# Attention scores of a two-layer decoder in 64-row products: heads by turns, three passes, and two bias transfers

## The chip, the cores and the metric

The kernel runs on one core of a Trainium2 chip. The metric is the device time of one execution in microseconds (us). Five engines work side by side, each through its own instructions in order: TensorE (PE; its weight loads are shown apart, as PEld), VectorE (DVE), ScalarE (ACT), GpSimd (POOL) and SyncE (SP), which here only issues transfers.

## What is computed

Two decoder layers over 256 positions of width 1024. Layer 0 mixes positions with a gated MLP, layer 1 with causal attention of 12 heads of 64. In both, 4 more heads of 64 attend to 256 memory tokens. Each layer ends in a SwiGLU block. Cut to what matters here:

```python
def memory_cross_attention(q_mem, mem, w_kv):            # 4 heads of 64, in both layers
    k, v = jnp.split(mem @ w_kv, 2, axis=-1)
    s = jnp.einsum('bshd,bmhd->bhsm', q, k) * HEAD_DIM ** -0.5
    return jnp.einsum('bhsm,bmhd->bshd', jax.nn.softmax(s, axis=-1), v)

# layer 0: u * (W_s v + b) by groups; layer 1: causal attention, 12 heads of 64
sub = jnp.concatenate([mix, mem_out], axis=-1) @ w_mix_out[i]
x = layer_norm(ALPHA * x + sub, ...)
x = layer_norm(ALPHA * x + swiglu(x, w_ffn_in[i], w_ffn_out[i]), ...)
```

## The kernel before, in words

Every large product is made of three passes. An operand is split into a rounded part hi and a rest lo, and hi·hi + lo·hi + hi·lo is added up in one PSUM tile. The helper `split` does that: ScalarE copies hi (L376), VectorE subtracts to get lo (L377). Weights are streamed from memory by SP in blocks of 128 x 2048, in an order written out by hand, split half by half (`spl_...` tiles), and used by PE (`mm`, L401). PE's order is that of the code. The orders of VectorE, ScalarE and SP are three long tables of numbers, `VECTOR_ORDER`, `SCALAR_ORDER` and `SYNC_ORDER`, which `keep_order` turns into dependencies.

The stages by time in the profile: the v projection of layer 0 (`va`, from 5.5 us), memory queries `hqm`, the u projections `pu`, memory keys `hkm`, the gating products `sv`, the memory scores `sm` (near 58 us), output projection `opa` (from 64 us), the feed-forward block (104 to 272 us, tiles Xf, Zf, fof and others), then layer 1: values `bv`, queries `hqm`, memory scores `sm` (near 303 us), six rounds of `qk` projection, scores `s`, transposes `pt` and `pv` (300 to 363 us), output projection `opc`, and the second feed-forward block (to 545 us).

The scores are the place of the change. Heads come in pairs, since two heads of 64 fill 128 rows. The scores do not use three passes over 64 rows. `stack_q` (L628, L629) writes, for each head of a pair, a tile whose one half of the rows holds hi and whose other half holds lo of the head's queries, times 0.125. `stack_k` (L636, L637, L638) writes the keys' hi into both halves of one tile and their lo into one half of another, `klm`, whose other half POOL has set to zero once at the start (L426). Two products over 128 rows then give all three terms: stacked queries by doubled hi keys, and stacked queries by `klm`. Every step of the stacking works on 64 rows: for a pair, two ScalarE and two VectorE steps for the queries, four ScalarE and two VectorE steps for the keys. In layer 1 this is done for six pairs (`qks`, by `qk_half`; `scores` issues 8 products a pair), in both layers for two pairs of memory heads (`qqm`, `kkm`; `mem_scores` issues 16 products a layer). The softmax then runs on VectorE and ScalarE, `pt` or `ptm` turns the result, and `pv` or `pvm` multiplies it with the values, two heads to a tile, in products 64 columns wide.

The gating of layer 0 adds a bias, `bs`. It is loaded by four transfers that spread one row over 64 partitions each, beside one transfer for the gating weights `wsT`. The tile `mix` holds the mixer's results, split, for the output projection.

Of the kernel before, what the change touches and what calls it, by code (L numbers as in the profile page):

```python
# [21 lines left out]
P = 128  # L22
D = 1024
T = 256
# [15 lines left out]
NEG = -1e30  # L40
BIG = 3e38
# [151 lines left out]
class Stream:  # L193
# [27 lines left out]
    def load_ahead(self):  # L221

        while self.loaded < len(self.units):
            name, n = self.units[self.loaded]
            tag = self.tag(name)
            if tag:
                if tag in self.held:
                    return
                self.held.add(tag)
                raw = self.actp.tile([P, 2, D], F32, tag=tag, name=f"raw_{name}").rearrange("p a c -> p (a c)")  # L230
            else:
                if sum(self.left[r] > 0 for r in self.ring) >= RAW_BUFS:
                    return
                self.ring.append(name)
                raw = self.rawp.tile([P, 2048], F32, tag="raw", name=f"raw_{name}")
            self.raw[name] = raw
            self.nc.sync.dma_start(raw[:, :n], self.unit_ap(block(name)))
            self.loaded += 1
# [80 lines left out]
)  # L319
SCALAR_ORDER = (  # L320
# [882 lines left out]
```

## Time and profile before

| | |
|---|---|
| time, median of 3 runs | 562.05 us (561.79 to 562.11) |
| the profiled execution | 561.61 us, span from first to last instruction 559.9 us |
| PE busy | 549.4 us, 98%, 3035 products |
| DVE busy | 504.6 us, 90%, 697 instructions |
| ACT busy | 388.1 us, 69%, 605 instructions |
| POOL busy | 48.4 us, 9% |
| transfers | 121.01 MB, mean 216 GB/s |

In the profile a name such as `s<-qks` is the tile written and the tiles read. `128*64` behind a product is the part of the array, rows by columns, that holds its weights. Products overlap, so the length of one is longer than the distance to the next. The chain is the work that ended last, followed back from the end, each step to what released it.

### The profile page before, as it was taken

The numbers are of one execution on the slowest core, as the hardware profiler recorded it, in microseconds if no ns is written. First come the engines' busy times: TensorE is split into PE (matmuls) and PEld (weight loads), VectorE is DVE, ScalarE is ACT, GpSimd is POOL, SyncE is SP. The second block draws the span as 40 slices with busy tenths as digits, with TensorE's granted clock in tenths as the row PEclk, the third lists the DMA queues.
The fourth block names the chain that finished last, engine by engine and source line by source line (L and its number), as shares of the span: only waits on it lengthen the run. The fifth ranks groups of instructions, "written<-read, shape, count | busy, mean of one in ns | idle before, by whom it ended". The sixth has DMA issues, their size and how long they took to land.

```text
span 559.9 us, 8132 instructions
## 1 busy us (share of the span) xinstructions
PE 549.4 (98%) x3035; PEld 475.6 (85%) x3035; DVE 504.6 (90%) x697; ACT 388.1 (69%) x605; POOL 48.4 (9%) x61
## 2 busy tenths in 40 slices
PE   9999999999999999999999999999999999999994
PEld 8999779988888888888899989787888888888884
DVE  5889957799998999999998878768999999999997
ACT  4767749975867769585466998768767687767720
POOL 1011002010202011100000000000202020201001
PEclk9999999999999999999999999999999999999998
DMA  8998665437969968778568243553379887988802
GB/s 304 384 382 289 245 266 123 178 63 174 292 173 331 250 247 202 267 222 323 165 244 357 77 151 121 145 122 142 66 222 274 294 214 244 271 238 249 253 6 77
DMA packets 23464, 121.01 MB, mean 216 GB/s; under 512 B 2688, under 2 KB 4736, under 8 KB 13312
## 3 DMA queue, kind: packets, MB, share of 16 engines
q1 hardware_dynamic: 17088, 99.16, 47.2%
q0 software_dynamic: 5760, 20.97, 21.0%
q8 instruction: 24, 0.39, 0.3%
q10 hardware_dynamic: 576, 0.34, 0.2%
q14 instruction: 16, 0.13, 0.1%
HBM read 119.42 MB, written 1.05 MB: 215 GB/s over the span
## 4 chain that ended last, share of the span: by engine, by line
PE 84%; DMA 6%; DVE 5%; issue 2%; ACT 2%; SPq 0%; POOLq 0%; POOL 0%; ACTq 0%; DVEq 0%
PE fof L401 11%; PE Xg L401 10%; PE Xf L401 10%; PE fog L401 9%; PE Zf L401 7%; PE Zg L401 7%; PE qk L401 6%; PE opc L401 4%; PE opa L401 3%; PE bv L401 3%; DMA raw_o<-in_w 2%; PE pg L401 2%; PE pf L401 2%; DMA raw_qm<-in_w 2%; PE pvm L401 2%
## 5 line engine op out<-in xcount | busy, mean ns | idle before, releaser
L376 ACT CAST spl_s_M<-raw_s_T 128x1024 fp32r<-128x1024 f32 x80 | 82.1, 1051 | 30.4 <-DVE raw_s_T L255 27.6
L377 DVE TENSOR_TENSOR spl_s_M<-raw_s_T,spl_s_M 128x1024 fp32r<-128x1024 f32 x80 | 95.9, 1219 | 2.1 <-ACT spl_s_M L376 2.1
L376 ACT CAST spl_s_M<-raw_s 128x1024 fp32r<-128x1024 f32 x60 | 61.5, 1051 | 19.0 <-DMA raw_s<-in_w 13.6
L377 DVE TENSOR_TENSOR spl_s_M<-raw_s,spl_s_M 128x1024 fp32r<-128x1024 f32 x60 | 71.3, 1220 | 3.3 <-ACT spl_s_M L376 3.3
L401 PE MATMUL fof<-spl_w,htf 128*128 128x512 f32 x264 | 63.0, 391 | 0.0
L401 PEld LDWEIGHTS fof<-spl_w,htf 128*128 128x128 f32 x264 | 49.4, 188 | 10.1
L377 DVE TENSOR_TENSOR spl_w<-raw_w,spl_w 128x1024 fp32r<-128x1024 f32 x44 | 53.5, 1220 | 0.9 <-ACT spl_w L376 0.9
L401 PE MATMUL fog<-spl_w,htg 128*128 128x512 f32 x228 | 54.2, 390 | 0.0
L401 PEld LDWEIGHTS fog<-spl_w,htg 128*128 128x128 f32 x228 | 42.8, 188 | 8.8
L255 DVE TENSOR_TENSOR raw_s_T<-raw_s_T,raw_s 128x1024 f32<-128x1024 f32 x40 | 48.3, 1220 | 0.2
L376 ACT CAST spl_w<-raw_w 128x1024 fp32r<-128x1024 f32 x44 | 45.7, 1053 | 0.1
L401 PE MATMUL qk<-x2T,spl_qk 128*128 128x256 f32 x288 | 36.6, 284 | 0.0
L219 POOL DMA_DIRECT2D raw_s<-in_w x20 | 17.1, 856 | 217.3 <-DVE spl_s_M L377 139.9
L401 PEld LDWEIGHTS qk<-x2T,spl_qk 128*128 128x128 f32 x288 | 35.2, 192 | 0.6 <-DVE klm L638 0.4
L401 PE MATMUL Xg<-spl_s_M,SgM 128*128 128x512 f32 x120 | 29.4, 394 | 0.0
L401 PE MATMUL Xf<-spl_s_M,SfM 128*128 128x512 f32 x120 | 29.3, 394 | 0.0
L401 PE MATMUL Xg<-spl_s_M,x3T 128*128 128x512 f32 x120 | 29.3, 392 | 0.0
L401 PE MATMUL Xf<-spl_s_M,x1T 128*128 128x512 f32 x120 | 28.9, 390 | 0.0
L401 PE MATMUL Zf<-spl_s_M,SfM 128*128 128x512 f32 x120 | 28.8, 390 | 0.0
L401 PE MATMUL Zg<-spl_s_M,SgM 128*128 128x512 f32 x120 | 28.8, 390 | 0.0
L401 PEld LDWEIGHTS Xg<-spl_s_M,x3T 128*128 128x128 f32 x120 | 22.4, 188 | 5.4 <-DVE x3T L377 0.4
L219 POOL DMA_DIRECT2D raw_s_T<-in_w x20 | 17.3, 865 | 108.9 <-DVE mb L551 74.7
(264 smaller groups left out, 1102.8 us busy)
## 6 DMA issues: line engine op xcount, KB each, us to landing
raw_w<-in_w SPq DMA_DIRECT2D x22, 1024.0 KB, 6.8
raw_s<-in_w SPq DMA_DIRECT2D x20, 1024.0 KB, 6.9
raw_s_T<-in_w SPq DMA_DIRECT2D x10, 1024.0 KB, 5.3
raw_s_T<-in_w POOLq DMA_DIRECT2D x20, 512.0 KB, 7.5
raw_s<-in_w POOLq DMA_DIRECT2D x20, 512.0 KB, 5.6
raw_o<-in_w SPq DMA_DIRECT2D x8, 1024.0 KB, 8.3
raw_qk<-in_w SPq DMA_DIRECT2D x6, 1024.0 KB, 4.8
raw_v<-in_w SPq DMA_DIRECT2D x7, 512.0 KB, 7.6
```

What stands on the lines that cost most here:

```text
L219: self.nc.gpsimd.dma_start(self.raw[name][:, sl], self.unit_ap(other)[:, sl], accum_op=ALU.add)
L255: self.nc.vector.tensor_add(raw, raw, self.raw[used[1]][:, sl])
L376: nc.scalar.copy(hi, src)
L377: nc.vector.tensor_sub(lo, src, hi.bitcast(F32))
L401: nc.tensor.matmul(o, lhsT, rhs, start=start, stop=stop, skip_group_check=on)
```

## The change

The stacking goes. `split_q` writes hi and lo of a pair's queries, both heads at once, in one ScalarE and one VectorE step over 128 rows, and `split` does the same for the keys. The scores are three passes (hi·hi, lo·hi, hi·lo) over 64 rows each: head 0 of the pair lies on rows 0 to 63, head 1 on rows 64 to 127, and the products of the two heads alternate, each into its own score tile. A pair in layer 1 takes 12 products where it took 8, the memory heads of a layer 24 where they took 16. `klm` and its two memsets on POOL go. VectorE has 20 instructions fewer, ScalarE 40 fewer. In `mem_scores` the softmax of a pair starts after the products of both heads.

The bias is spread over the partitions ahead of the launch: two thirds of it stand behind the gating weights and come in their transfer, the rest in one of its own, so five transfers become two. Three weight blocks, `qm0`, `u0` and `km0`, are loaded in two halves each, so SP's count stays the same. The three tables are new throughout; their numbers tell nothing by themselves.

```diff
+IN_HALVES = ("qm0", "u0", "km0")
...
-            self.nc.sync.dma_start(raw[:, :n], self.unit_ap(block(name)))
+            parts = 2 if name in IN_HALVES else 1
+            for x in range(parts):
+                sl = slice(x * n // parts, (x + 1) * n // parts)
+                self.nc.sync.dma_start(raw[:, sl], self.unit_ap(block(name))[:, sl])
...
 SYNC_ORDER = (
-    0, 1, 2, 3, 4, 5, 7, 6, 8, 9, 10, 11, 15, 16, 12, 17, 21, 13, 19, 18, 24, 23, 14, 22, 25, 26, 20, 27, 28, 29, 33,
+    1, 0, 2, 3, 4, 18, 5, 6, 7, 8, 9, 11, 10, 22, 12, 13, 14, 16, 15, 19, 17, 23, 20, 24, 25, 26, 21, 27, 28, 29, 32,
...
-        klm = const.tile([P, 2, 2, T], F32R, name="klm")
-        for par in range(2):
-            nc.gpsimd.memset(klm[HD - HD * par:2 * HD - HD * par, :, par, :].bitcast(F32), 0.0)
...
-        def mem_scores(qa, k, nm, psum_tile):
-            ka, kl = k
+        def mem_scores(qa, ka, nm, psum_tile):
             pr = []
-            for h in range(4):
-                c, par = h // 2, h % 2
-                s = psum_tile[h](f"s{nm}{h}")
-                for lo in range(2):
+            for c in range(2):
+                ss = [psum_tile[2 * c + par](f"s{nm}{2 * c + par}") for par in range(2)]
+                for n, (a, b) in enumerate(LO_LAST):
                     for q in range(2):
-                        mm(s[:, q * 256:(q + 1) * 256], qa[c][:, par, q * P:(q + 1) * P], (kl[:, c] if lo else ka[c])[:, par, :],
-                           not lo and not q, bool(lo and q))
-                pr.append(Softmax(s, [(0, 256), (256, 512)], f"{nm}{h}"))
+                        for par, s in enumerate(ss):
+                            mm(s[:, q * 256:(q + 1) * 256], qa[c][rows(par), a, q * P:(q + 1) * P], ka[c][rows(par), b, :],
+                               not n and not q, bool(n == 2 and q))
+                pr += [Softmax(s, [(0, 256), (256, 512)], f"{nm}{2 * c + par}") for par, s in enumerate(ss)]
...
-        def stack_q(qa, t):
-
-            for par in range(2):
-                own, other = rows(par)
-                nc.scalar.mul(qa(par)[own], t[own], 0.125)
-                nc.vector.scalar_tensor_tensor(qa(par)[other], t[own], 0.125, qa(par)[own].bitcast(F32),
-                                               ALU.mult, ALU.subtract)
-
-        def stack_k(ka, kl, t):
-
-            for par in range(2):
-                own, other = rows(par)
-                nc.scalar.copy(ka(par)[own], t[own])
-                nc.scalar.copy(ka(par)[other], t[own])
-                nc.vector.tensor_sub(kl[own, par], t[own], ka(par)[own].bitcast(F32))
+            return slice(HD * par, HD * par + HD)
+
+        def split_q(hi, lo, t):
+
+            nc.scalar.mul(hi, t, 0.125)
+            nc.vector.scalar_tensor_tensor(lo, t, 0.125, hi.bitcast(F32), ALU.mult, ALU.subtract)
...
-        nc.sync.dma_start(wsT, ins["wsT"])
+        nc.sync.dma_start(wbig, ins["wsT"])
...
-        for t, c, g0, g1 in ((wbig, 12 * P, 0, 4), (vbig, 12 * P, 4, 6)):
-            for j in range(2):
-                nc.sync.dma_start(t[j * HD:(j + 1) * HD, c:c + (g1 - g0) * P].rearrange("p (g t) -> p g t", t=P),
-                                  ins["bs"][j:j + 1, g0:g1, :].to_broadcast([HD, g1 - g0, P]))
+        nc.sync.dma_start(vbig[:, 12 * P:14 * P], ins["bs"])
...
-                stack_q(lambda par: st[:, 0, par, :], t)
+                split_q(qks[hp][:, 0, 0, :], qks[hp][:, 0, 1, :], t)
...
-                stack_k(lambda par: st[:, 1, par, :], kl, t)
+                split(qks[hp][:, 1, 0, :], qks[hp][:, 1, 1, :], t)
...
-            for lo in range(2):
-                for par, s in enumerate(ss):
-                    q, k = st[:, 0, par, :], kl[:, par, :] if lo else st[:, 1, par, :]
-                    mm(s[:, 0:128], q[:, 0:128], k[:, 0:128], not lo, False)
-                    mm(s[:, 128:384], q[:, 128:256], k, False, bool(lo))
+            for n, (a, b) in enumerate(LO_LAST):
+                for c0, c1, q0, k1 in ((0, 128, 0, 128), (128, 384, 128, 256)):
+                    for par, s in enumerate(ss):
+                        mm(s[:, c0:c1], st[rows(par), 0, a, q0:q0 + P], st[rows(par), 1, b, :k1], not n and not c0, bool(n == 2 and c0))
```

Where instructions stand before and after, at the three places that the prediction speaks of. A row is a line of the code, the instruction, the tile written, the tiles read and the shape. First PE in layer 1, the scores of the first pair of heads, before. `s_2987` and `s_2988` are the score tiles of its two heads, `qks` holds the stacked queries and the doubled keys, `klm` the keys' low parts:

```order
L401 MATMUL s_2987<-qks_2861 128x128
L401 MATMUL s_2987<-qks_2861 128x256
L401 MATMUL s_2988<-qks_2861 128x128
L401 MATMUL s_2988<-qks_2861 128x256
L401 MATMUL s_2987<-klm,qks_2861 128x128
L401 MATMUL s_2987<-klm,qks_2861 128x256
L401 MATMUL s_2988<-klm,qks_2861 128x128
L401 MATMUL s_2988<-klm,qks_2861 128x256
```

The same place in the changed kernel, the first of three passes and the start of the second:

```order
L403 MATMUL s_2968<-qks_2842 128x128
L403 MATMUL s_2969<-qks_2842 128x128
L403 MATMUL s_2968<-qks_2842 128x256
L403 MATMUL s_2969<-qks_2842 128x256
L403 MATMUL s_2968<-qks_2842 128x128
L403 MATMUL s_2969<-qks_2842 128x128
```

Eight products head by head have become three passes of four, in which each product is followed by the other head's.

Then VectorE in layer 0 around the gating, before. `klm<-hkm` are stack_k's subtractions, `gt` the gating, `spl_o` splits of the output projection's weights, `mix` the splits of the gating's result:

```order
L377 TENSOR_TENSOR spl_o_2_0_888<-raw_o_2_605,spl_o_2_0_888 128x1024
L377 TENSOR_TENSOR spl_o_2_1_925<-raw_o_2_605,spl_o_2_1_925 128x1024
L377 TENSOR_TENSOR spl_o_3_0_955<-raw_o_3_743,spl_o_3_0_955 128x1024
L638 TENSOR_TENSOR klm<-hkm_586,kkm_584 64x256
L965 TENSOR_TENSOR gt_684<-sv_675,wsT 128x512
L967 TENSOR_TENSOR gt_684<-gt_684,uT_452 128x512
L965 TENSOR_TENSOR gt_700<-sv_691,wsT 128x512
L638 TENSOR_TENSOR klm<-hkm_586,kkm_584 64x256
L965 TENSOR_TENSOR gt_716<-sv_707,vn 128x512
L638 TENSOR_TENSOR klm<-hkm_586,kkm_585 64x256
L377 TENSOR_TENSOR mix_1_670<-gt_684,mix_1_670 128x256
L377 TENSOR_TENSOR mix_0_669<-gt_684,mix_0_669 128x256
```

and in the changed kernel, where `kkm<-hkm` are the two full-height splits of the keys:

```order
L947 TENSOR_TENSOR gt_669<-sv_660,wsT 128x512
L379 TENSOR_TENSOR kkm_577<-hkm_579,kkm_577 128x256
L949 TENSOR_TENSOR gt_669<-gt_669,uT_445 128x512
L947 TENSOR_TENSOR gt_685<-sv_676,wsT 128x512
L947 TENSOR_TENSOR gt_701<-sv_692,vn 128x512
L949 TENSOR_TENSOR gt_701<-gt_701,uT_563 128x512
L949 TENSOR_TENSOR gt_685<-gt_685,uT_504 128x512
L379 TENSOR_TENSOR spl_o_2_0_881<-raw_o_2_598,spl_o_2_0_881 128x1024
L379 TENSOR_TENSOR kkm_578<-hkm_579,kkm_578 128x256
L379 TENSOR_TENSOR spl_o_0_1_847<-raw_o_0_466,spl_o_0_1_847 128x1024
L552 TENSOR_REDUCE mm_759<-sm_743 128x2
L379 TENSOR_TENSOR mix_2_656<-gt_685,mix_2_656 128x256
```

The gating and the first keys have moved ahead of spl_o_2_0, spl_o_0_1, spl_o_2_1 and spl_o_3_0, which now stand among and behind them; spl_o_3_0 and spl_o_3_1 come after the splits of mix_0 to mix_5.

Last SP at the start, before. `raw_v` is the first weight block, whose first 256 columns hold x and the others the weights of v; `mraw` is memory:

```order
L438 DMA raw_v_138<-in_w 128x256
L438 DMA raw_v_138<-in_w 128x384
L440 DMA raw_v_138<-in_w 128x1024
L440 DMA raw_v_181<-in_w 128x1024 x2
L440 DMA raw_v_218<-in_w 128x1024
```

and in the changed kernel:

```order
L435 DMA raw_v_135<-in_w 128x384
L435 DMA raw_v_135<-in_w 128x256
L437 DMA raw_v_135<-in_w 128x1024
L437 DMA raw_v_178<-in_w 128x1024 x2
L894 DMA mraw_310<-in_memT 128x2x256
L437 DMA raw_v_215<-in_w 128x1024 x2
```

The part with x is now issued second, and the first block of memory has moved ahead of the later blocks of v.

More of the change, by code (lines that the diff above doesn't have):

```diff
@@ L621, in rows @@
         def rows(par):
-            return slice(HD * par, HD * par + HD), slice(HD - HD * par, 2 * HD - HD * par)
-        def stack_q(qa, t):
-            for par in range(2):
-                own, other = rows(par)
-                nc.scalar.mul(qa(par)[own], t[own], 0.125)
-                nc.vector.scalar_tensor_tensor(qa(par)[other], t[own], 0.125, qa(par)[own].bitcast(F32),
-                                               ALU.mult, ALU.subtract)
-        def stack_k(ka, kl, t):
-            for par in range(2):
-                own, other = rows(par)
-                nc.scalar.copy(ka(par)[own], t[own])
-                nc.scalar.copy(ka(par)[other], t[own])
-                nc.vector.tensor_sub(kl[own, par], t[own], ka(par)[own].bitcast(F32))
+            return slice(HD * par, HD * par + HD)
+        def split_q(hi, lo, t):
+            nc.scalar.mul(hi, t, 0.125)
+            nc.vector.scalar_tensor_tensor(lo, t, 0.125, hi.bitcast(F32), ALU.mult, ALU.subtract)
         def proj_t(name, xs):
@@ L649, in mem_q @@
             for c in range(2):
-                stack_q(lambda par: qa[c][:, par, :], t[:, c, :])
+                split_q(qa[c][:, 0, :], qa[c][:, 1, :], t[:, c, :])
             return qa
@@ L656, in mem_k @@
             for c in range(2):
-                stack_k(lambda par: ka[c][:, par, :], klm[:, c], t[:, c, :])
-            return ka, klm
+                split(ka[c][:, 0, :], ka[c][:, 1, :], t[:, c, :])
+            return ka
         def acc_mms(acc, lhs, rhs, first, last):
@@ L1036, in qk_half @@
             if j == 0:
-                st = actp.tile([P, 2, 512], F32R, tag="hm", name=f"qks{hp}", bufs=4).rearrange("p a (b t) -> p a b t", b=2)
-                qks[hp] = st, klm[:, hp % 2]
-                stack_q(lambda par: st[:, 0, par, :], t)
+                qks[hp] = actp.tile([P, 2, 512], F32R, tag="hm", name=f"qks{hp}", bufs=4).rearrange("p a (b t) -> p a b t", b=2)
+                split_q(qks[hp][:, 0, 0, :], qks[hp][:, 0, 1, :], t)
             else:
                 stream.done(f"qk{hp}")
-                st, kl = qks[hp]
-                stack_k(lambda par: st[:, 1, par, :], kl, t)
+                split(qks[hp][:, 1, 0, :], qks[hp][:, 1, 1, :], t)
         def scores(hp):
-            st, kl = qks[hp]
+            st = qks[hp]
             ss = [acc_tile(f"s{hp}{par}") for par in range(2)]
-            for lo in range(2):
-                for par, s in enumerate(ss):
-                    q, k = st[:, 0, par, :], kl[:, par, :] if lo else st[:, 1, par, :]
-                    mm(s[:, 0:128], q[:, 0:128], k[:, 0:128], not lo, False)
-                    mm(s[:, 128:384], q[:, 128:256], k, False, bool(lo))
+            for n, (a, b) in enumerate(LO_LAST):
+                for c0, c1, q0, k1 in ((0, 128, 0, 128), (128, 384, 128, 256)):
+                    for par, s in enumerate(ss):
+                        mm(s[:, c0:c1], st[rows(par), 0, a, q0:q0 + P], st[rows(par), 1, b, :k1], not n and not c0, bool(n == 2 and c0))
             return [Softmax(s, [(0, 128), (128, 384)], f"b{hp}{j}", flat(mask)) for j, s in enumerate(ss)]
@@ L1171, in _pack @@
         blk[f"qk{i}"] = _cols(np.concatenate([q, k], axis=1), 0, KT, 0, 256)
+    bs = np.repeat(inp["a_b_s"][0].reshape(6, 2, P).transpose(1, 0, 2).reshape(2, -1), HD, axis=0)
     flat = np.concatenate([blk[n].reshape(-1) for n, _ in weight_blocks()])
@@ L1176, in _pack @@
         "memT": np.ascontiguousarray(inp["mem"][0].T),
-        "wsT": np.ascontiguousarray(inp["a_w_s"][0].transpose(2, 0, 1)),
-        "bs": np.ascontiguousarray(inp["a_b_s"][0].reshape(6, 2, P).transpose(1, 0, 2)),
+        "wsT": np.concatenate([inp["a_w_s"][0].transpose(2, 0, 1).reshape(P, -1), bs[:, :4 * P]], axis=1),
+        "bs": np.ascontiguousarray(bs[:, 4 * P:]),
         "a_ln_v": np.concatenate([inp["a_ln_v_g"], inp["a_ln_v_b"]], axis=1),
```

112 rows, old and new, of tables (SCALAR_ORDER, SYNC_ORDER, VECTOR_ORDER) are left out of this document.

## The prediction

> **What bounds the kernel now.** I read the page's engine table first, then the windows, then the chain of work that ended last. The engine table and the chain's shares by engine:
>
> ```profile
> PE 549.4 (98%) x3035; PEld 475.6 (85%) x3035; DVE 504.6 (90%) x697; ACT 388.1 (69%) x605; POOL 48.4 (9%) x61
> ...
> PE 84%; DMA 6%; DVE 5%; issue 2%; ACT 2%; SPq 0%; POOLq 0%; POOL 0%; ACTq 0%; DVEq 0%
> ```
>
> PE is the bound, VectorE the next. A busy PE need not be at its pace, so I take the pace from the chain, whose pieces are start, length, engine, line and count:
>
> ```profile
> 302.73 1.45 PE sm L401 x12
> 304.19 0.71 PE sm L401 x4
> ...
> 310.67 0.93 PE s L401 x8
> ...
> 319.78 2.87 PE qk L401 x24
> ...
> 322.65 0.81 PE pv L401 x8
> ...
> 355.47 0.92 PE s L401 x8
> ```
>
> A 128x256 product at full pace takes 2.87/24 = 0.12 us. The eight score products of a pair of heads, half of them 128 wide, take 0.92 to 0.93, so 0.115 each: a narrow one is hardly cheaper. The 16 memory scores of layer 1 take 1.45 + 0.71 = 2.16, where 16 x 0.12 would be 1.92.
>
> Two stretches from the windows (PE, PEld, DVE, ACT, POOL busy; clock; DMA share; GB/s) say where nothing is to be had:
>
> ```profile
> 10.00:20.00 10.00, 10.00 (x60) 10.00 (x59) 7.19 (x11) 6.76 (x12) 0.00 (x0) 1.00 1.02 407
> 125.00:256.00 131.00, 131.00 (x597) 108.92 (x597) 127.49 (x126) 94.59 (x114) 13.39 (x16) 1.00 0.83 241
> ```
>
> In the feed-forward stretch PE never rests, and VectorE is busy 127.5 of 131 us: what is won before it is kept, since VectorE's work there is released by PE's, but nothing is won in it. So the change is worth what it does to PE's own work in the scores, and to the few waits beside them. The largest lie in layer 0. PE's timeline there (start, length, idle before):
>
> ```profile
> 57.77 0.40 PE L401 MATMUL sm<-kkm,qqm 128*128 128x256 f32 x2
> ...
> 61.60 3.04 PE L401 MATMUL pvm<-spl_vm,memT 128*128 128x256 f32 x24
> 64.47 4.72 PE L401 MATMUL opa<-spl_o,mix 128*128 128x512 f32 x20
> 69.63 2.60 PE L401 MATMUL opa<-spl_o,mix 128*128 128x512 f32 x10 [0.44 <-DVE mix L377]
> ```
>
> The 16 memory scores last from 57.77 to 61.60, 3.83 us, twice their 1.92. And 20 products of opa begin at 64.47, end by 69.19, and 0.44 passes until VectorE's mix is there. The chain of the same stretch says why:
>
> ```profile
> 55.94 0.42 DVE klm L638
> ...
> 58.77 0.37 ACT kkm L636
> ...
> 60.37 0.38 ACT kkm L637
> ...
> 60.77 0.44 DVE klm L638
> ...
> 69.15 0.43 DVE mix L377
> ```
>
> From 55.94 to 61.21 the chain runs through the four half-height subtractions of stack_k (0.42 to 0.44 each) and ScalarE's copies (0.37, 0.38) in turn: PE waits for each head's stacked keys.
>
> **Scores on PE: 16 products become 24, 8 become 12.** All hangs on whether a product on rows 0 to 63 and its neighbour on rows 64 to 127 run side by side. The trace of before has no 64-row product. It has the nearest thing, products 64 columns wide (pv), and PE's timeline in a window of 0.12 us shows two of them:
>
> ```profile
> 322.38 0.28 PE L401 MATMUL qk<-x2T,spl_qk 128*128 128x256 f32 x1
> 322.58 0.44 PE L401 MATMUL pv<-pT,vt 128*64 128x256 f32 x2
> ```
>
> and one of them, in the groups by form (busy, mean ns), lasts 405 ns:
>
> ```profile
> L401 PE MATMUL pv<-pT,vt 128*64 128x256 f32 x24 | 4.0, 405 | 0.0
> ```
>
> Two together last 0.44, hardly longer than one; and the eight of a burst take 0.81 us. Two neighbours on different parts of the array do overlap here, on columns. I take it that they do on rows, since the code lets the heads alternate and gives each its own score tile. The same rows price the change of shape: the last full-height product starts at 322.38, pv at 322.58, 0.20 instead of 0.12, so 0.08 is lost on the way in. I put the whole visit at 0.3 us, my estimate: that 0.08, as much on the way out, and something for the first products on each side, whose weights I suppose cannot be loaded ahead. The Trainium skill ("TensorEngine Tiling (Array Packing)", Key Properties) says that changing the tiling mode drains TensorE; the 0.08 agrees.
>
> Side by side, a pair of attention heads costs six slots of 0.115 = 0.69, with the visit 0.99, against 0.92: +0.07, over six pairs +0.4 us. The ends: -1.4 (no visit to pay) and +4.6 (no overlap: 12 x 0.115 + 0.3 - 0.92 = 0.76 each). Memory scores of layer 1: 12 x 0.12 + 0.3 = 1.74 against 2.16, -0.4 (ends -0.7 and 24 x 0.12 + 0.3 - 2.16 = +1.0). Layer 0: 1.74 plus 0.1 left of the waits, against 3.83: -2.0 (ends -2.4 and -0.6).
>
> What loads weights is the weak point. From the tile's own view (count, then least, median and largest ns):
>
> ```profile
> L401 PEld LDWEIGHTS s<-qks x24: 187/192/193, 310.4 to 355.5; 128*128 128x128 f32 x24
> ...
> L628 ACT ACTIVATE qks<-qk x12: 362/378/379, 302.8 to 347.9; 64x256 fp32r<-64x256 f32 x12
> L629 DVE SCALAR_TENSOR_TENSOR qks<-qk,qks x12: 417/422/427, 303.2 to 348.8; 64x256 fp32r<-64x256 f32 x12
> L636 ACT CAST qks<-qk x12: 365/367/370, 307.8 to 353.5; 64x256 fp32r<-64x256 f32 x12
> L637 ACT CAST qks<-qk x12: 363/366/371, 308.2 to 353.9; 64x256 fp32r<-64x256 f32 x12
> L638 DVE TENSOR_TENSOR klm<-qk,qks x12: 404/422/428, 308.6 to 354.3; 64x256 fp32r<-64x256 f32 x12
> ```
>
> Each score product loads 128 columns in 0.19 us (overlapped, one per 0.115). The Trainium skill ("TensorE: Matmul & The Clock Gate", LDWEIGHTS) speaks against the change: a load costs its columns over 1.2, here 107 ns, whatever its rows, so halving the rows makes no load cheaper, and if two halves cannot load at once, 12 loads are 1.28 us a pair. By that the six pairs alone would cost 2.2 us more than now. No run here shows it for rows; the overlap of pv is on columns.
>
> **The splits.** A step over all 128 rows costs what the half costs, since mix is split from a product in just that form:
>
> ```profile
> L377 DVE TENSOR_TENSOR mix<-pv,mix 128x256 fp32r<-128x256 f32 x6 | 2.5, 422 | 2.6 <-ACT mix L376 2.5
> ...
> L376 ACT CAST mix<-pv 128x256 fp32r<-128x256 f32 x6 | 2.2, 371 | 1.5 <-PE pv L401 1.4
> ```
>
> So in layer 1's pairs VectorE drops from 24 steps to 12, 12 x 0.42 = 5.1 us, and ScalarE from 36 to 12, 24 x 0.37 = 8.9 us. Almost all of it lies beside PE's work and is worth nothing. On the path it takes the chain of layer 0 above (counted) and loosens two stalls. One is the 0.44 at 69.63: four subtractions of 0.42 become two there, and in the order shown above the mix splits come ahead of the splits of spl_o_3_0 and spl_o_3_1, which stood before the last of them, so I take -0.4 (ends 0 and -0.6). The other is in layer 1, where the transposes waited for VectorE:
>
> ```profile
> L1060 PE MATMUL pt<-ident,pb 128*128 128x128 f32 x36 | 5.1, 274 | 0.7 <-DVE mix L377 0.7
> ```
>
> I count -0.4 of 0.7 (ends 0 and -0.8), the rest as a new wait on VectorE's other order. In mem_scores the first reduction now waits for both heads' 12 products instead of 4, at most 0.5 us later; the softmax is read by PE only some 10 us later, so zero.
>
> **The transfers and the new order.** The bias transfers are read from 56 us on, the klm memsets on POOL were waited for by nobody, and the second table load that ScalarE's order now has falls at 10 to 20 us, where ScalarE was busy 6.8 of 10: zero each, hidden by PE's 96 products of va. If that cover were gone, the table load would cost its own length of about 1.3 us:
>
> ```profile
> 1.24 1.28 ACT L397 ACT_TABLE_LOAD   x1 [1.24 <-PEq L1192]
> ```
>
> Halves of qm0, u0 and km0 land earlier than needed: zero. The very start is not hidden. SP now issues the x part of the first block second. The timeline of the start:
>
> ```profile
> 0.80 0.87 SPq L438 DMA_DIRECT2D raw_v<-in_w  x2
> ...
> 4.72 0.29 DVE L441 CAST x0T<-raw_v 128x256 fp32r<-128x256 f32 x1 [3.72 <-DMA raw_v<-in_w]
> ...
> 5.46 1.01 PE L401 MATMUL va<-spl_v,x0T 128*128 128x384 f32 x2 [0.28 <-DVE x0T L442]
> ```
>
> Two issues take 0.87, so x is asked for 0.44 later; PE waited for just this operand, and is full from here on. I take +0.4 (ends 0, if the landing does not follow the issue, and +0.6).
>
> **Sum.** +0.4 (start) -2.0 (layer 0 scores) -0.4 (its stall) -0.4 (layer 1 memory scores) +0.4 (six pairs) -0.4 (pt) = -2.4 us. The profiled execution took 561.61 us (span 559.9); the sum makes it 559.2. The median of the runs is 562.05, 0.44 above it; I forecast **559.65**. With visits of 0.2 or 0.4 us (eight of them, 0.8 either way) and both stalls gone or kept (0.6 and 0.8) it reaches 558.25 and 561.25.
>
> **Rivals.** *The halves run one after the other* (weights or products): 12 x 0.115 a pair. With visits +4.6, layer 1 memory +1.0, layer 0 -0.6, start +0.4, pt -0.4 is +5.0; without visits +2.8, +0.7, -0.9, +0.4, -0.4 is +2.6. That is 564.65 to 567.05, middle 565.8. For it: the load time does not shrink with rows. Against: pv's pairs. It decides from where a pair's burst passes 0.92 + 2.8/6 = 1.39 us, which eats all other gains. Chance 0.20.
>
> *VectorE keeps layer 0.* PE finishes the scores 2 us earlier and waits for mix instead, since gt, the splits of spl_o and mix are one queue on VectorE. Then both terms of layer 0 go: -2.4 + 2.4 = 0, 562.05. For it: the chain there ends in DVE mix; against: that queue loses steps and the new order moves spl_o_3_0 and spl_o_3_1 behind mix. Chance 0.15.
>
> *No price for the visit and all stalls gone.* 0 -2.4 -0.6 -0.7 -1.4 -0.8 = -5.9, 556.15; some of it, about 558, is likelier than all. Chance 0.12.
>
> **Numbers.** Forecast 0.53, rivals 0.20, 0.15 and 0.12. A measurement of this kernel can tell about 0.2%, 1.1 us, from no change. Of the forecast 0.47 is faster and 0.06 within; the third rival is faster; of the second 0.02 is faster, 0.11 within, 0.02 slower; of the first 0.01 is within and 0.19 slower. That gives faster 0.61, same 0.18, slower 0.21. The range, 557.8 to 566.2, leaves out the lower half of the third rival and the upper half of the first, 0.16; the forecast's own is 558.25 to 561.25.
>
> **What would show it.** Right: pairs of s and sm products some 10 ns apart in PE's timeline, a burst of 12 near 1.0 us, the memory scores of layer 0 below 2.2 us, va starting 0.2 to 0.5 later, no idle before opa. Wrong: s products about 0.1 us apart and a burst above 1.3; or sm short but a wait for mix before opa; or a burst of 0.7, which would mean that the visit costs nothing.

## The result, and the profile after

The changed kernel takes 558.27 us (median of 5 runs, 557.63 to 559.76), the kernel before 561.79 (561.38 to 562.11). The ratio is 0.9941, 95% interval 0.9926 to 0.9957: 0.6% faster, a small gain that is clear of the noise. In a second group of runs it was 558.16 against 561.27, ratio 0.9944 (0.9931 to 0.9957). The profiled execution took 558.43 us, span 556.7, against 561.61 and 559.9.

The engine table and the chain's shares of the profile after:

```profile
PE 547.4 (98%) x3075; PEld 472.1 (85%) x3075; DVE 492.0 (88%) x677; ACT 372.0 (67%) x566; POOL 45.3 (8%) x59
...
PE 92%; issue 3%; DVE 2%; DMA 2%; SPq 1%; POOL 0%; ACT 0%; POOLq 0%
```

PE still is the bound, and its share of the chain rose from 84% to 92%. That is the first hint of what was won: not shorter work on PE, which is busy 2.0 us less with 40 products more, but stretches in which the chain ran elsewhere. PE's timeline over layer 0's memory scores (start, length, group):

```profile
57.57 0.40 PE L403 MATMUL pvm<-spl_vm,memT 128*128 128x256 f32 x2
57.90 1.69 PE L403 MATMUL sm<-kkm,qqm 64*128 64x256 f32 x24
59.52 3.13 PE L403 MATMUL pvm<-spl_vm,memT 128*128 128x256 f32 x24
62.49 6.99 PE L403 MATMUL opa<-spl_o,mix 128*128 128x512 f32 x30
69.32 1.91 PE L584 MATMUL ptm<-ident,pm 128*128 128x128 f32 x16
```

From the first score to the next product it is now 1.62 us (57.90 to 59.52), where it was 3.83. The 30 products of opa stand in one group, so the 0.44 between its first 20 and last 10 is gone. The chain of the same stretch used to run through VectorE and ScalarE; now it stays on PE:

```profile
54.90 3.07 PE pvm L403 x24
57.97 1.62 PE sm L403 x24
59.59 3.06 PE pvm L403 x24
62.65 6.83 PE opa L403 x30
```

The same pieces in layer 1, memory scores and two attention pairs:

```profile
299.77 1.62 PE sm L403 x24
301.39 5.94 PE qk L403 x48
307.33 0.89 PE s L403 x12
308.22 3.07 PE qk L403 x24
...
315.82 0.88 PE s L403 x12
```

24 products of 64 rows take 1.62 where 16 of 128 rows took 2.16. A pair takes 0.89 where it took 0.93 with 8 products, but the qk behind it takes 3.07 where 24 such products took 2.87: the way back to full height is paid there. Pair and qk together went from 3.80 (0.93 + 2.87) to 3.96. The qk behind the memory scores shows the same, 5.94 where the chain before has

```profile
304.91 5.76 PE qk L401 x48
```

Two products at the start of a burst, and the loads of their weights:

```profile
315.75 0.33 PE L403 MATMUL s<-qks 64*128 64x128 f32 x2
```

```profile
315.75 0.18 PEld L403 LDWEIGHTS s<-qks 64*128 64x128 f32 x2 [0.17 <-issue]
```

The tile's own view of the same loads and products (count, then least, median and largest ns):

```profile
L403 PEld LDWEIGHTS s<-qks x72: 182/186/188, 307.3 to 352.7; 64*128 64x128 f32 x72
L403 PE MATMUL s<-qks x72: 217/326/333, 307.3 to 352.7; 64*128 64x128 f32 x36, 64*128 64x256 f32 x36
```

Two products of up to 0.33 us last 0.33 together, two loads of 0.18 last 0.18 together: the two halves of the array work side by side in both.

Two more things moved. The transposes of layer 1 wait no longer, and the second feed-forward block begins with a wait that was not there. Its row among the groups, and the chain that leads to it:

```profile
L1039 PE MATMUL pt<-ident,pb 128*128 128x128 f32 x36 | 5.0, 274 | 0.0
...
L403 PE MATMUL pg<-spl_r_A,x3T 128*128 128x512 f32 x24 | 6.2, 394 | 0.3 <-DVE x3T L379 0.3
```

```profile
385.70 1.15 DVE spl_s_M L379
386.85 0.02 issue
386.87 1.23 DVE raw_s_T L259
388.10 0.61 DVE x3T L379
388.71 0.04 issue
388.75 3.47 PE pg L403 x14
```

PE arrives some 3.4 us earlier than before and needs x3T, which VectorE makes behind two long weight steps (1.15 and 1.23).

### The profile page after: what moved, and what is told of

Same layout as the page of the kernel before. It is cut to its first block, busy times and chain, and to the rows that moved or that the text cites. A ratio compares the mean times of both kernels' runs of the same rounds, so it can differ in the third digit from the quotient of the medians.

```text
span 556.7 us, 8132 instructions
## 1 busy us (share of the span) xinstructions
PE 547.4 (98%) x3075; PEld 472.1 (85%) x3075; DVE 492.0 (88%) x677; ACT 372.0 (67%) x566; POOL 45.3 (8%) x59
## 4 chain that ended last, share of the span: by engine, by line
PE 92%; issue 3%; DVE 2%; DMA 2%; SPq 1%; POOL 0%; ACT 0%; POOLq 0%
PE fof L403 11%; PE Xf L403 10%; PE Xg L403 9%; PE fog L403 9%; PE Zg L403 7%; PE Zf L403 7%; PE qk L403 6%; PE opa L403 4%; PE pu L403 3%; PE bv L403 3%; PE pvm L403 3%; PE opc L403 2%; PE hkm L403 2%; PE hqm L403 2%; PE pf L403 2%
## 5 line engine op out<-in xcount | busy, mean ns | idle before, releaser
L403 PEld LDWEIGHTS Zf<-spl_s_M,SfM 128*128 128x128 f32 x120 | 22.5, 188 | 4.7
```

Source lines behind the costliest of these rows:

```text
L403: nc.tensor.matmul(o, lhsT, rhs, start=start, stop=stop, skip_group_check=on)
```

## The experiments

The theory, W: the products by turns make the scores neither cheaper nor dearer by much; the gain is waits that went, because splits of queries and keys take half as many steps. Rivals: P, the overlap of the products is the gain; O, the new order of the three queues is the gain; D, the transfers are part of it. All ratios are to the kernel before, which took 561.27 to 561.40 us in the groups of runs, with 95% intervals.

| run | median us | ratio |
|---|---|---|
| changed kernel again | 558.16 | 0.9944 (0.9931 to 0.9957) |
| x first | 558.25 | 0.9941 (0.992 to 0.9962) |
| old transfers | 557.92 | 0.9947 (0.9935 to 0.9959) |
| heads apart | 560.63 | 0.999 (0.998 to 1.0001) |
| two visits | 560.65 | 0.9986 (0.9974 to 0.9999) |
| scores beside pv | 559.50 | 0.9958 (0.9943 to 0.9972) |
| old order | 560.46 | 0.9982 (0.9968 to 0.9996) |
| half steps, old order | 561.84 | 1.001 (1.0001 to 1.0019) |
| stacked pairs, old order | 559.33 | 0.9969 (0.9957 to 0.998) |
| half steps, new order | 569.09 | 1.0135 (1.012 to 1.015) |
| stacked pairs, new order | 568.28 | 1.0114 (1.0088 to 1.0139) |
| kernel before, new order | 576.46 | 1.0282 (1.0261 to 1.0303) |

The run of the changed kernel again, the reference of its group:

> The changed kernel once more, as the reference of this group: 557.8 to 558.7, and the kernel before 561.2 to 561.8.

It came out so, 558.16 against 561.27.

**The turns of the heads.** In both kinds of scores the loop over the heads goes outside:

```diff
-            for n, (a, b) in enumerate(LO_LAST):
-                for c0, c1, q0, k1 in ((0, 128, 0, 128), (128, 384, 128, 256)):
-                    for par, s in enumerate(ss):
+            for par, s in enumerate(ss):
+                for n, (a, b) in enumerate(LO_LAST):
+                    for c0, c1, q0, k1 in ((0, 128, 0, 128), (128, 384, 128, 256)):
```

> The changed kernel with one edit: the products of a pair are issued head by head, not by turns; the other engines keep their work and their order. Theory W (the gain over the kernel before is made of waits that went; the overlap of the two heads only keeps the added products from costing more): without turns nothing overlaps, 12 products of 0.115 are 1.38 us a pair where a burst now takes 0.89, so +0.5 to +0.7 for each of six pairs (+3.0 to +4.2), and +1.3 for each layer's 24 memory scores (2.88 against 1.62): 558.3 becomes 563.9 to 565.1, slower than the kernel before. Rival Q (the array overlaps products on different rows in whatever order they come, or the order of issue does not matter): within 0.5 of 558.3. Rival P (the overlap itself is the gain of 3.5 us and nothing else is): about 561.8.

It took 560.63: 2.4 us more than the changed kernel's 558.2, less than half of what W expected. PE's timeline at the pair from 315.82 on, in two cuts of it:

```profile
315.82 0.67 PE L403 MATMUL s<-qks 64*128 64x128 f32 x4
```

```profile
315.82 1.29 PE L403 MATMUL s<-qks 64*128 64x128 f32 x12
317.04 1.22 PE L403 MATMUL qk<-x2T,spl_qk 128*128 128x256 f32 x8
```

The burst from first score to next product is 1.22 where it was 0.89 (315.75 to 316.64), so +0.33, eight bursts 2.6. The four products that had begun by 316.16 began at 315.82, 315.98, 316.15 and 316.16: the last two only 7 ns apart. In PE's queue the first six belong to head 0, on rows 0 to 63, and the next six to head 1. But the product that signals the end of head 0's six is the eighth to begin, at 316.44: two of head 1's, on the other rows, began ahead of it. It is the same in all six pairs. So the halves overlap in part without turns. W's direction held, its price was too high; Q's 0.5 is exceeded, and P's 561.8 is not met either. Without turns most of the gain would be gone: overlap is what keeps the added products from costing 2.4 us.

**The price of a visit.** The burst of pairs 0 to 4 is cut in two by six of the qk products that follow anyway:

```diff
             for n, (a, b) in enumerate(LO_LAST):
+                if n == 1 and between:
+                    between()
...
-                prs[i - 1] = scores(i - 1)
+                head = acc_tile(f"qk{i}1")[:, :T].rearrange("p (j t) -> p j t", j=1)
+                prs[i - 1] = scores(i - 1, lambda: ws_proj(head, f"qk{i}", xs, (1,), (0, 2)))
```

> The changed kernel with the burst of each of pairs 0 to 4 cut in two: after the first pass (4 products) come 6 of the 24 full-height qk products that follow anyway, then the other 8 score products. No work is added, only 5 more visits to the 64-row shape. Theory W, in which a visit costs 0.28 to 0.45 us in way in, first products and way out: +1.4 to +2.3, so 559.7 to 560.6. Rival F (a visit is nearly free, as the bursts of 0.89 against six slots of 0.115 suggest for the 0.2 that the chain shows, and what was lost at the pairs has another cause): within 0.5 of 558.3.

It took 560.65, 2.4 more than the x-first run beside it. PE's timeline at the second pair:

```profile
315.27 0.85 PE L1043 MATMUL pt<-ident,pb 128*128 128x128 f32 x6 [0.37 <-DVE pb L563]
316.05 0.50 PE L403 MATMUL s<-qks 64*128 64x128 f32 x4
316.47 0.98 PE L403 MATMUL qk<-x2T,spl_qk 128*128 128x256 f32 x6
317.39 0.73 PE L403 MATMUL s<-qks 64*128 64x128 f32 x8
318.04 1.22 PE L403 MATMUL qk<-x2T,spl_qk 128*128 128x256 f32 x8
```

From 316.05 to 318.04 are 1.99 us; less six qk products at 0.12 that is 1.27, where one burst took 0.89: a visit costs 0.38 us. Five are 1.9, and the new wait of 0.37 at the transposes makes 2.3. Theory W's 0.28 to 0.45 holds (the time came out a hair above its 560.6) and F falls.

**Scores beside pv.** Can a visit be shared? Four pairs' scores go between the halves of their round's qk, with pv straight behind. The orders of VectorE and ScalarE follow at a few places:

```diff
-            ws_proj(t, f"qk{hp}", xs, (j,))
+            ws_proj(t, f"qk{hp}", xs, (j,), (0, 4))
+            if between:
+                between()
+            ws_proj(t, f"qk{hp}", xs, (j,), (4, KT))
```

> The changed kernel with the scores of pairs 1 to 4 moved behind the first 12 of the 24 qk products of their round, and the pv products (64 columns wide) straight behind the scores, then the other 12 qk products: one way out and one way in fewer in each of 4 rounds, no work changed. Theory W with a way in or out at 0.1 to 0.2 us: -0.4 to -1.0, so 557.3 to 557.9. Rival: changing from half the rows to half the columns costs as much as both ways, or pv now waits for ScalarE's copies of the transposes: 558.3 to 559.5.

It took 559.50, 1.25 more than the x-first run, so the rival came out. The first such round:

```profile
314.71 1.56 PE L403 MATMUL qk<-x2T,spl_qk 128*128 128x256 f32 x11
...
316.31 0.96 PE L403 MATMUL s<-qks 64*128 64x128 f32 x12
317.20 0.88 PE L403 MATMUL pv<-pT,vt 128*64 128x256 f32 x8
318.01 1.69 PE L403 MATMUL qk<-x2T,spl_qk 128*128 128x256 f32 x12
319.54 0.38 PE L584 MATMUL ptm<-ident,pm 128*128 128x128 f32 x2
```

From 314.71 to 319.54 are 4.83 us; in the changed kernel the same 24 + 12 + 8 products stand from 315.75 to 320.51, 4.76 by its timeline. Going from half rows to half columns saves nothing over going by full height. Later rounds have two waits at the transposes (0.16 and 0.29); the rest of the 1.25 I did not trace.

**Steps and order, apart.** The changed kernel with the old order of all three queues (the three tables alone differ):

> The changed kernel with the order of VectorE, ScalarE and SyncE of the kernel before: each instruction stands where it stood there, a full-height split where the first of its halves stood. Theory W: the steps that went are what counts, so most of the gain stays; the order decides only the smaller stalls (0.7 before opa, 0.4 at the second feed-forward's start either way): 558.0 to 559.4, the memory scores of layer 0 under 2.2 us. Rival O (the new order is what made it faster): 560.5 to 562.

The same with the splits in half-height steps again, each where its half stood before:

```diff
-            nc.scalar.mul(hi, t, 0.125)
-            nc.vector.scalar_tensor_tensor(lo, t, 0.125, hi.bitcast(F32), ALU.mult, ALU.subtract)
+            for par in range(2):
+                r = rows(par)
+                nc.scalar.mul(hi[r], t[r], 0.125)
+                nc.vector.scalar_tensor_tensor(lo[r], t[r], 0.125, hi[r].bitcast(F32), ALU.mult, ALU.subtract)
...
-                split(qks[hp][:, 1, 0, :], qks[hp][:, 1, 1, :], t)
+                split_k(qks[hp][:, 1, 0, :], qks[hp][:, 1, 1, :], t)
```

> The changed kernel's products, but the splits of queries and keys in half-height steps, and the three queues in the order of the kernel before, each half where the half stood there. It differs from the run with the old order by the half steps alone (20 more on VectorE, 20 on ScalarE), and from the kernel before by the products (64-row, by turns) and 20 fewer ScalarE copies. Theory W: the waits of the kernel before are all back (2 us at the memory scores of layer 0, 0.7 before opa, 0.7 at the transposes), and only PE's own part is left: +0.9 at the six pairs, -0.4 at the memory scores of layer 1: 561.4 to 562.6. Rival P (the products by turns are the gain): as the old order's run, 559.5 to 560.5.

And the change at the memory scores alone, with the attention pairs stacked as before:

```diff
-                split_q(qks[hp][:, 0, 0, :], qks[hp][:, 0, 1, :], t)
+                stack_q(lambda par: st[:, 0, par, :], t)
...
-                split(qks[hp][:, 1, 0, :], qks[hp][:, 1, 1, :], t)
+                stack_k(lambda par: st[:, 1, par, :], kl, t)
```

> The change made at the memory scores alone: their products and splits as changed; the six attention pairs of layer 1 in the stacked form with its 8 products of 128 rows; the queues in the order of the kernel before. Against the run with the old order it has the pairs' change undone: PE's 6 x 0.15 come back as a gain, the 0.7 at the transposes as a loss. Theory W: within 0.5 of the old order's run (559.5 to 560.5), so 559.2 to 560.6; against the kernel before -1.5 to -2.5. Rival (the pairs' part is a gain of its own): over 560.8.

Half steps in the old order, with all the new products and 20 fewer key copies on ScalarE, take 561.84, inside W's range, where the kernel before takes 561.27: the products by turns alone gain nothing (P falls). Full-height steps in the same order take 560.46, 1.4 less by the medians of two groups, 2.0 by the spans (560.0 and 558.0; both profiles begin the memory queries at 22.6). So the steps are worth that, but W promised more: its range for the old order's run, 558.0 to 559.4, was missed by 1.1 us, and the median stands at the edge of rival O's 560.5 to 562. The memory scores of that run are short, as W held, in its chain:

```profile
57.39 1.62 PE sm L403 x24
```

PE's timeline of the half-step run shows where the first of it lies:

```profile
57.36 1.09 PE L404 MATMUL sm<-kkm,qqm 64*128 64x256 f32 x13
58.74 1.23 PE L404 MATMUL sm<-kkm,qqm 64*128 64x256 f32 x11 [0.29 <-ACT kkm L379]
59.90 3.12 PE L404 MATMUL pvm<-spl_vm,memT 128*128 128x256 f32 x24
```

The memory scores last 2.54 us (57.36 to 59.90) and wait for keys in the middle; with full-height steps they last the 1.62 above. They lasted 3.83 before, so about 0.9 of the 2.2 is owed to the half steps, and the rest to what this run keeps of the change: four key copies fewer on ScalarE and the shorter burst, which were not taken apart. The wait for mix before opa (0.3) is back as well, and layer 1's memory scores take 1.37 + 0.74 in its chain:

```profile
301.34 1.37 PE sm L404 x17
302.72 0.74 PE sm L404 x6
```

That is 0.9 + 0.5 + 0.5 = 1.9 of the 2.0, taking the 0.5 at opa from the shift of what follows.

The stacked pairs in the old order take 559.33, inside W's range and 1.9 less than the kernel before. By the medians that is a little less than the old order's run (560.46; the two intervals just overlap, 0.9968 to 0.9996 and 0.9957 to 0.998); the profiled spans of the two are equal, 558.0 each. So the attention pairs' part of the change is no gain of its own, and by the medians may be a loss of up to a microsecond: what the visits cost and the wait that goes at the transposes cancel, or nearly. That wait, with stacked pairs, then with half steps:

```profile
L1066 PE MATMUL pt<-ident,pb 128*128 128x128 f32 x36 | 5.1, 274 | 0.7 <-DVE mix L381 0.7
```

```profile
L1048 PE MATMUL pt<-ident,pb 128*128 128x128 f32 x36 | 4.9, 272 | 0.0
```

With stacked pairs it stays, with half-height steps on VectorE (as many as before) it goes. Both ends of the wait moved. Counted from layer 1's first memory score, PE begins these transposes 0.47 us later in the half-step run than in the kernel before (35.16 against 34.69), as three pairs that cost 0.16 more each would make it, and VectorE's mix is ready 0.63 earlier (35.15 against 35.78). What made mix earlier is open: ScalarE's 12 doubled key copies are gone, but that was not tried by itself.

The order's own part is what is left: 560.46 to 558.16, 2.3 us by the medians, 1.3 by the spans (558.0 to 556.7). The spans hold chance from the start, since the old order's profile begins the memory queries 0.4 to 0.6 earlier; from there on the changed kernel's two profiles are 1.7 and 1.9 shorter. Some of it is a wait in the second feed-forward block, which the changed kernel lacks:

```profile
L403 PE MATMUL Xg<-spl_s_M,SgM 128*128 128x512 f32 x120 | 29.5, 395 | 0.6 <-ACT u2g L743 0.6
```

The kernel before, in that same order, lacks this wait as well:

```profile
L401 PE MATMUL Xg<-spl_s_M,SgM 128*128 128x512 f32 x120 | 29.4, 394 | 0.0
```

So it is no fault of the old order by itself: it comes where that order stands on the changed program. From its first Zg product to its first of `last`, the second feed-forward block takes 147.3 us with the old order on the changed program, 146.4 in the kernel before and 146.7 in the changed one. Another 0.7 lies between the start of the first feed-forward block and layer 1's first qk and was not traced. And some is the end. From the last step of VectorE to the end of the span all four runs with the old order take 3.2 to 3.4 us, all ten with the new order 2.6. SP's last stores, in the kernel before and in the changed one:

```profile
552.08 4.36 SPq L498 DMA_DIRECT2D out<-xres  x4
```

```profile
547.72 6.14 SPq L495 DMA_DIRECT2D out<-xres  x4
```

In the new order the first half's rows are stored 4.4 us earlier on the clock, 1.2 earlier relative to the span's end, so they no longer stand close before the last store. That this is what shortens the end is argued, not tried.

**The new order with more steps.** Three runs: the half-height steps and the stacked pairs by the edits above, and the program before with the tables of the changed one. In all three the loop over the halves is cut in two, so that the extra steps stand right beside their partners, ScalarE's copies of both halves ahead of both subtractions:

> The changed kernel with its products, but the splits of queries and keys done in half-height steps again: 20 steps more on VectorE and 20 more on ScalarE, each half right behind its partner in the order. Theory W: the waits come back where VectorE or ScalarE is ahead of PE by little. Layer 0: each of the two key splits is done two steps later (0.42 + 0.37), so the memory scores take 2.4 to 3.2 us instead of 1.62; some of the 0.7 before opa and of the 0.9 at the transposes of layer 1 comes back. +1.2 to +2.8, so 559.5 to 561.1. Rival P (the gain is PE's overlap): within 0.4 of 558.3, since PE's products are untouched. Rival O (the gain is the new order of the three queues): within 0.4 of 558.3 too, since the order is kept.

> The changed kernel with the old form for the six attention pairs of layer 1 alone: stacked queries and doubled keys, 8 products of 128 rows, 12 more steps on VectorE and 24 on ScalarE; memory scores as changed. Theory W: PE's work gets shorter by 6 x 0.16 = 0.95, and the stall at the transposes of pair 0 (0.7 to 0.9) comes back with VectorE's steps: 557.3 to 558.6. Rival P (the overlap made the pairs cheaper): 558.8 to 560. If the steps cost nothing in this stage: 557.3.

> The kernel before with the order of the three queues of the changed kernel: the half-height splits stand together where the full-height one stands. Theory W: the half steps are all still there, so the memory scores of layer 0 still wait and take 3 to 4 us: 561 to 563. Rival O (the order is the gain): 558 to 559.5.

569.09, 568.28 and 576.46: all far beyond what either theory gave. The waits of PE in layer 1 in the last of them (engine and line that waited, releaser, us in total, times, longest):

```profile
PE pt L1064 <- DVE pb L566: 5.3, 3, 2.0
PE s L401 <- ACT qks L639: 1.0, 2, 0.7
PE s L401 <- DVE klm L642: 0.7, 1, 0.7
```

PE waits 5.3 us for softmax steps (pb) of VectorE and 1.7 for queries' and keys' splits, where the changed kernel has no wait in this stage. That is less than half of the 18 us by which this run is longer than the changed kernel; the rest was not traced. So steps and order are not two gains to be added. The order's 1.3 to 2.3 us were had only together with the change of steps, and these three runs say nothing of what a step costs in an order made for it. Whether an order made anew for the kernel before would gain as much was not tried. Theories W and O both failed here: each took the order for something that could be moved over.

**Transfers and start.**

```diff
-IN_HALVES = ("qm0", "u0", "km0")
+IN_HALVES = ()
...
-        nc.sync.dma_start(vbig[:, 12 * P:14 * P], ins["bs"])
+        for t, c, g0, g1 in ((wbig, 12 * P, 0, 4), (vbig, 12 * P, 4, 6)):
+            for j in range(2):
...
 SYNC_ORDER = (
-    1, 0, 2,
+    0, 1, 2,
```

The upper part is one kernel, in which SP's numbers follow the transfers; the lower (x first) is another.

> The changed kernel with the bias in four spreading transfers beside the gating weights and no block loaded in halves, as before the change. Forecast and theory W: nothing waits for them, so within 0.3 of the changed kernel. Rival D (the transfers gave part of the gain): 0.5 or more slower.

> The changed kernel with the first two transfers of SyncE's queue in the old order, x first. The forecast counted +0.4 for their exchange: by that this kernel is 0.4 faster, 557.9. Theory W (PE begins 0.38 later but makes it up within the first 20 us, since later blocks set its pace there): va begins 0.3 to 0.4 earlier and the memory queries at the same time as now within 0.1; 558.2 to 558.4.

557.92 and 558.25, both the same as the changed kernel: D falls, and so does the forecast's +0.4. PE's first product of va, changed kernel and x first:

```profile
5.84 2.33 PE L403 MATMUL va<-spl_v,x0T 128*128 128x384 f32 x11 [1.21 <-DVE x0T L438]
```

```profile
5.37 2.91 PE L403 MATMUL va<-spl_v,x0T 128*128 128x384 f32 x12 [0.18 <-DVE x0T L439]
```

That looks like the forecast's 0.4, but the other runs with the changed kernel's first two transfers begin va between 5.36 and 5.68, so most of it is chance. W's time came out, its reason did not: the memory queries begin 0.42 earlier with x first (22.76 against 23.18), where W had them at the same time within 0.1. That too is inside the scatter of the start: they begin between 22.26 and 23.18 in the nine runs with the exchange, between 22.61 and 23.14 in the five without.

No version here beat the changed kernel by more than the noise.

## Why the prediction was right, point by point

Forecast 559.65, measured 558.27, inside the range, and just inside the forecast's own part of it, 558.25 to 561.25; faster, as held likeliest. The gain was forecast at 2.4 us and measured 3.5. The mechanism was right (halves side by side, waits gone, visits paid); several terms were off, and that they fell on both sides is luck: gains left out or put too small, and the start's cost that did not come, are worth 2.1 us; costs put too small or not foreseen take 1.1 back.

- **Start, +0.4: zero.** The memory queries begin at 23.18 in the profile after, 23.14 before. The exchange of two transfers moves nothing that stands out of the start's scatter. The step that failed was "I take +0.4": the landing was taken to follow the issue, and PE to be full from va on.
- **Layer 0's memory scores, -2.0: -2.0**, that is -2.2 for the burst and 0.2 for the ways in and out. The largest term, and right.
- **The stall before opa, -0.4: -0.8.** The 0.44 went, and about 0.3 of unevenness in the same stretch.
- **Layer 1's memory scores, -0.4: -0.3**, 2.16 to 1.62 with 0.09 more ahead and 0.18 behind (5.94 for the qk that took 5.76): right.
- **Six pairs, +0.4: about +0.95** (3.96 against 3.80 each). The visit was put at 0.3 and measured 0.38. The six slots were priced at 0.115, 0.69 together; 0.89 with 0.2 more in the qk behind makes 1.09, less 0.38 is 0.71: right. The mis-sized term is the visit.
- **The transposes, -0.4: -0.9**, the wait of 0.7 and what it delayed. The reason failed: VectorE's fewer steps were not needed, since the run with half-height steps, as many as before, has no such wait; there PE came 0.47 later and mix 0.63 earlier.
- **Not forecast:** the end, -0.6, and small waits ahead of layer 1, -0.2; and the new wait at the second feed-forward block with what lies around it, +0.5. The prediction had "the rest" of the stall at the transposes return as a wait on VectorE's other order; none came there, and the one that did come stands one stage later. The terms as measured sum to -2.0 - 0.8 - 0.3 + 0.95 - 0.9 - 0.2 + 0.5 - 0.6 = -3.35, and the spans differ by 3.2.

The largest omission is the order itself. The forecast read the three tables for the stalls it knew and gave them no term of their own; the runs give them 1.3 to 2.3 us of the 3.1 to 3.5.

The rival in which the halves run one after the other falls by the pairs of products and loads. The Trainium skill ("TensorE: Matmul & The Clock Gate", the section on LDWEIGHTS) prices a load by its columns whatever its rows, and the trace agrees as to the rows (186 ns at 64 rows, 192 before at 128), though each is recorded with 186 ns and not with the rule's 107. In the second pair's burst a new pair of loads begins every 0.108 to 0.121 us. The same page ("Part 3: Packing small matmuls") lets a load overlap products of another row group and has the products of different tiles start some 4 ns apart. The trace agrees: in the changed kernel the two products of a pair mostly start 3 ns apart, and so do their two loads. VectorE keeping layer 0 falls by the chain, which stays on PE. No price for the visit falls by the cut bursts. (The range's upper end, 566.2, was to leave out the upper half of the first of these rivals, whose middle is 565.85; nothing hangs on the difference.)

## What to carry to other kernels

Count the steps that feed a short burst before the products in it: here half as many splits were worth 1.4 to 2.0 us, and the new products by themselves nothing. A burst in another tiling shape has a fixed price for the way in and out (0.38 us here), so it pays when it is long or when it takes a wait away, not when it only saves a few slots. An order tuned by hand belongs to its program: test a change of work in the old order before judging either, and look there for waits that neither program has in its own order (0.6 us here).

## What the runs showed of the hardware

- 64-row products of one half of the array start ahead of earlier ones of the other half: with six of head 0 queued ahead of six of head 1, head 1's first began about 0.34 us after head 0's first, next to its third, and the product that ends head 0's six was the eighth to begin, in all six pairs. The Trainium skill ("TensorE: Matmul & The Clock Gate", "Part 3: Packing small matmuls") has products start strictly in program order; the recorded starts of this run say otherwise. Turns were worth 0.33 us a burst, not the 0.5 to 0.7 expected.
- A visit to the 64-row shape costs 0.38 us, measured by cutting bursts in two, and going on to the 64-column shape directly costs as much as by way of full height (4.83 against 4.76 us for the same products).
